# An MLP by Strassen's seven products, with hidden operands through DRAM

## The chip, the core and the metric

The kernel runs on one core of a Trainium2 chip. A core has a matrix engine (TensorE, PE in the profile; its weight loads are PEld), a vector engine (VectorE, DVE), a scalar engine (ScalarE, ACT), GpSimd (POOL) and a sync engine (SyncE, SP) whose queue issues most DMAs here. Each engine works through its own list of instructions in order and waits on semaphores of the others. The metric is device time in microseconds of one launch.

## The reference

One layer (`DEPTH` is 1) on 1024 rows of 1024 channels: a mixer of two recurrences, then an MLP with 4096 hidden channels, then a last norm. Everything is float32.

```python
for l in range(DEPTH):
    h = rms_norm(x, norm_mix[l])
    x = x + hybrid_mixer(h, ...)          # eight projections, two recurrences, gates, @ w_out
    h = rms_norm(x, norm_mlp[l])
    x = x + jnp.square(jax.nn.relu(h @ w_up[l])) @ w_down[l]
return rms_norm(x, norm_final)
```

`w_up` is 1024 x 4096, `w_down` 4096 x 1024. The change touches the MLP, the output projection of the second half of the rows and the norm between them.

## The kernel before

Time (1024 rows) is worked on in two chunks of `T` = 512. Products in float32 are made of three passes of the matrix engine: `split` (lines 72 to 74) makes a high part with a ScalarE copy into the type `float32r` (line 73) and a low part with a VectorE subtraction (line 74), and `mm3` (lines 113 to 116) issues high x high, high x low and low x high into one PSUM bank. So each operand that TensorE reads costs ScalarE and VectorE one pass, and each product of 128 x 128 x 512 costs three matmuls.

Weights lie in DRAM as tiles of 128 x 1024 floats (512 KB). `load_w` (line 79) puts a tile into one of three `raw` buffers by a DMA on SP's queue; `split_w` (line 84) makes the two parts, under a priority that puts it ahead of other work; `fill_w` and `get_w` (lines 96 and 103) run two tiles ahead of the use.

For each chunk the first norm is transposed and split into `hT`; four passes over channel groups run the projections, the recurrences and the gates and leave `y`, transposed and split. `out_proj` (line 598) multiplies `y` by `w_out`: for each half of 512 columns, four weight tiles, each used for two depth blocks and four blocks of 128 rows, so 192 matmuls for a chunk. For the second chunk it runs beside `second_norm(0)` (line 657), which norms the first chunk's rows, transposes them on TensorE into PSUM and splits them into `h20`; `second_norm(1)` then makes `h21` from the projection's results.

The MLP (from line 669) takes 512 hidden channels at a time, in eight blocks. For two groups of 256 channels it loads two tiles of `w_up` and two of `w_down`, forms `pu` in four PSUM banks (8 depth blocks x 2 chunks x 2 halves x 3 = 96 matmuls), and makes `u` = relu squared in two parts (lines 689 to 692). Then, for eight blocks of 128 rows, it forms `pd` in two banks (24 matmuls each) and VectorE adds it to `acc`, which holds the residual in SBUF (line 710). Up and down alternate block by block, and hidden values never leave SBUF. In the last block each row block is normed and stored as it ends (lines 711 to 722).

The order on each engine isn't the program's. A planner takes the traced program, with the order of the trace as priority (`high_priority(n)` moves a part up by n), and lists each engine's instructions by when it reckons their inputs and buffers to be ready; the chip then keeps that list. `tile_pool` hands out SBUF in stacks; a tag with `bufs=n` has n buffers that are used again when their last reader is done. PSUM has eight banks: tags `pj` (4), `sc` (2) and `hg` (2).

Of the kernel before, what the change touches and what calls it, by code (L numbers as in the profile page):

```python
# [10 lines left out]
F32 = mybir.dt.float32  # L11
# [7 lines left out]
P = 128  # L19
D = 1024  # L20
# [12 lines left out]
UP_TILES = 32  # L33
LEVELS = (2, 8)  # steps per segment; four segments are joined at a time

# columns of the per-channel parameters
# [5 lines left out]
def trunk(ctx: ExitStack, tc: tile.TileContext, x, wts, pv, gains, mask_f, mask_u, out):  # L42
# [4 lines left out]
    a2 = ctx.enter_context(tc.tile_pool(name="a2", bufs=4))  # L47
    wp = ctx.enter_context(tc.tile_pool(name="wp", bufs=3))
    ps = ctx.enter_context(tc.tile_pool(name="ps", bufs=1, space=PSUM))
    dram = ctx.enter_context(tc.tile_pool(name="dram", bufs=1, space=DRAM))  # L50

# [7 lines left out]
    up0 = MIX_TILES + OUT_TILES  # L59
    down0 = up0 + UP_TILES  # L60
    for b in range(8):
        seq += list(range(up0 + 4 * b, up0 + 4 * b + 4))
    ready, made = {}, [0]

    # at the start each engine's work goes in the order in which its inputs come in
# [10 lines left out]
    def raw_tile(name):  # L76
        return wp.tile([P, 1024], F32, tag="raw", name=name, bufs=3)
# [6 lines left out]
    def split_w(i, raw, pool, tag, bufs):  # L84
        h = pool.tile([P, 1024], F32R, tag=tag + "H", name=f"{tag}H{i}", bufs=bufs)
        lo = pool.tile([P, 1024], F32R, tag=tag + "L", name=f"{tag}L{i}", bufs=bufs)
        with tc.high_priority(400):
            split(raw, h, lo)
        return h, lo

    def load_split(i, pool, tag, bufs):
        return split_w(i, load_w(i), pool, tag, bufs)
# [3 lines left out]
    def fill_w(n):  # L96
        while made[0] < min(n, len(seq)):
            i = seq[made[0]]
            raw = raws.pop(0) if raws else load_w(i)
            ready[made[0]] = split_w(i, raw, wp, "w", 3)  # L100
            made[0] += 1
# [11 lines left out]
    def mm3(o, ah, al, bh, bl, first, last):  # L113
        PE.matmul(o, ah, bh, start=first, stop=False)  # L114
        PE.matmul(o, ah, bl, start=False, stop=False)  # L115
        PE.matmul(o, al, bh, start=False, stop=last)  # L116

# [30 lines left out]
    def a2_set(tag, name):  # L148
        return [
            [a2.tile([P, 4, T], F32R, tag=tag, name=f"{name}{q}{h}") for h in range(2)] for q in ("H", "L")  # L150
        ]
# [38 lines left out]
    def parameters():  # L190
        # softmax over the depth of one layer (exp(z) = sigmoid(z) / sigmoid(-z)), its running sum less the first, clipped
# [11 lines left out]
        # softplus(-lam) = max(-lam, 0) + 2 atanh(s / (2 - s)), s = sigmoid(-|lam|)  # L203
# [30 lines left out]
    def first_norm(c):  # L234
        dst = a2_set("h", f"hT{c}")
# [33 lines left out]
    def project(c, name):  # L269
        """256 channels, channels on partitions, a chunk of time along the free dimension."""  # L270
# [69 lines left out]
            # w = tanh(-log_a / 2): a = (1 - w) / (1 + w), sqrt(1 - a^2) = 2 sqrt(w) / (1 + w)  # L340
# [39 lines left out]
    def hgrn(c, p, q1, f, kk, v):  # L380
        """Two heads; decays from a step to the next are multiplied up, segment by segment."""
        nm = f"{c}{p}"
        mul = lambda o, a, b: V.tensor_tensor(out=o, in0=a, in1=b, op=ALU.mult)  # noqa: E731
# [3 lines left out]
        def blocks(rhs, name):  # L387
            """32 steps against themselves, 48 columns each."""
# [9 lines left out]
        # a step with itself and with the one before it in its pair  # L398
# [5 lines left out]
        # to segments of two  # L404
# [19 lines left out]
        for li, cw in enumerate(LEVELS):  # L424
# [13 lines left out]
            # decay from a segment's end to the last one's, and from the first one's start to a segment's  # L438
# [34 lines left out]
        # segments of 32, then of 64  # L473
# [41 lines left out]
        # the state at the start of each 128 steps, and what comes out  # L515
# [4 lines left out]
        for s in range(2):  # L520
# [7 lines left out]
            vn = lambda n: v[:, n, s * P : (s + 1) * P]  # noqa: B023, E731  # L528
# [3 lines left out]
            state = lambda n: scar[:, u, :] if n in (0, 4) else sn[:, n - 1, :]  # noqa: B023, E731  # L532
# [92 lines left out]
    for c in range(NC):  # L625
# [5 lines left out]
        ys = a2_set("y", f"y{c}")  # L631
# [15 lines left out]

# [1 line left out]
    late = ctx.enter_context(tc.tile_pool(name="late", bufs=1))  # L649
    gain1 = gain_tile(1)  # L650
    h2 = [a2_set("h", "h20")]
    acc = [late.tile([P, D], F32, tag="acc", name=f"acc{t}", bufs=8) for t in range(8)]
    for t in range(4):
        nc.sync.dma_start(acc[t], x2d[t])
        nc.sync.dma_start(acc[4 + t], x[(4 + t) * P : (5 + t) * P, :])
# [132 lines left out]
```

## Time and profile before

| | before |
|---|---|
| median of 3 runs | 1684.24 us (1683.9 to 1684.39) |
| profiled execution, first to last instruction (span) | 1682.1 us |
| of it before the second chunk's output projection | 926.7 us |
| last output projection, second norm, MLP, last norm | 755.4 us |
| instructions | 22982, of them 9624 matmuls |
| DMA moved | 133.24 MB, 79 GB/s in the mean |

The profile is of a single execution; its own time is given only as the span, and 2.1 us lie between that and the median of the runs. In the profile's lists a group of instructions has its line, engine, operation, the tile written and the tiles read (without buffer numbers), shapes, the number of instructions, then busy time in us and mean ns of one, then the idle time of the engine just before them with what ended it. A row of a window table is: from:to, length, then for PE, PEld, DVE, ACT and (where it worked) POOL the busy time in us with the number of instructions, then the granted clock, the DMA engines' busy share and GB/s. A row of the timeline is: start us, duration us, engine, line, operation, tiles, shapes, count, and in brackets what the engine had waited for.

### The profile page before, as it was taken

What the parts mean: (1) busy time and instruction counts of PE and PEld (TensorE: products, weight loads), DVE (VectorE), ACT (ScalarE), POOL (GpSimd) and SP (SyncE); (2) the same over time, 40 slices, a digit from 0 to 9 for tenths busy, and PEclk for the clock granted to TensorE, in tenths of its full rate; (3) what the DMA queues carried; (4) which work ended last, traced back from release to release, by engine and by line L of the source; (5) the groups of instructions that cost most, each with busy time, mean ns of one, the idle gap of its engine ahead of it and who ended that gap; (6) DMA issues with size and microseconds to landing.
All of it is one profiled execution on the core that took longest, in us unless ns stands there. A gap on an engine that the chain in (4) does not pass through costs nothing.

```text
span 1682.1 us, 22982 instructions
## 1 busy us (share of the span) xinstructions
PE 1652.1 (98%) x9624; PEld 1374.0 (82%) x9624; DVE 939.0 (56%) x1379; ACT 606.0 (36%) x974; POOL 61.8 (4%) x99
## 2 busy tenths in 40 slices
PE   7999999999999999999999999999999999999998
PEld 6788788787888787887887888888888888888886
DVE  5965947759646858658487663333424342424335
ACT  5534445435435435444363441212212121313132
POOL 0000100101000000000000000000000000000000
PEclk9999999999999999999999999999999999999999
DMA  6222222222353122122221531111111020202002
GB/s 217 88 72 92 89 76 89 76 89 87 101 172 116 64 93 96 65 87 88 86 90 64 188 112 38 53 49 38 63 38 63 26 75 26 75 26 76 26 0 100
DMA packets 38983, 133.24 MB, mean 79 GB/s; under 512 B 4576, under 2 KB 4704, under 8 KB 38880
## 3 DMA queue, kind: packets, MB, share of 16 engines
q1 hardware_dynamic: 38448, 130.21, 23.0%
q8 instruction: 75, 1.23, 0.3%
q10 hardware_dynamic: 432, 1.57, 0.3%
q14 instruction: 28, 0.23, 0.0%
HBM read 125.47 MB, written 6.29 MB: 78 GB/s over the span
## 4 chain that ended last, share of the span: by engine, by line
PE 84%; DVE 13%; issue 1%; DMA 1%; ACT 1%; POOL 0%; SPq 0%; DVEq 0%; POOLq 0%
PE pd L114 7%; PE pd L116 7%; PE pd L115 7%; PE pu L116 7%; PE pu L114 7%; PE pu L115 7%; DVE wL L74 2%; PE pj_ga L116 2%; PE pj_ga L115 2%; PE pj_ga L114 2%; PE pj_f L116 2%; PE pv L115 2%; PE pv L114 2%; PE pv L116 2%; PE pj_ma L116 2%; PE pj_ma L115 2%
## 5 line engine op out<-in xcount | busy, mean ns | idle before, releaser
L74 DVE TENSOR_TENSOR wL<-raw,wH 128x1024 fp32r<-128x1024 f32 x184 | 223.8, 1216 | 261.7 <-ACT wH L73 259.1
L73 ACT CAST wH<-raw 128x1024 fp32r<-128x1024 f32 x184 | 192.9, 1049 | 224.4 <-issue 65.4
L114 PE MATMUL pd<-dH,uH 128*128 128x512 f32 x512 | 199.2, 389 | 0.0
L115 PE MATMUL pd<-dL,uH 128*128 128x512 f32 x512 | 199.2, 389 | 0.0
L116 PE MATMUL pd<-dH,uL 128*128 128x512 f32 x512 | 199.2, 389 | 0.0
L710 DVE TENSOR_TENSOR acc<-pd,acc 128x512 f32<-128x512 f32 x128 | 87.2, 690 | 183.0 <-PE pd L116 183.0
L73 ACT CAST dH<-raw 128x1024 fp32r<-128x1024 f32 x32 | 33.6, 1052 | 281.7 <-PE pd L116 260.5
L116 PEld LDWEIGHTS pd<-dH,uL 128*128 128x128 f32 x512 | 96.1, 188 | 20.0
L115 PEld LDWEIGHTS pd<-dL,uH 128*128 128x128 f32 x512 | 96.1, 188 | 19.9
L114 PEld LDWEIGHTS pd<-dH,uH 128*128 128x128 f32 x512 | 96.1, 188 | 19.9
L691 DVE TENSOR_TENSOR r<-r 128x512 f32<-128x512 f32 x64 | 42.7, 686 | 114.8 <-ACT uH L690 114.8
L689 ACT ACTIVATE r<-pu 128x512 f32<-128x512 f32 x64 | 37.7, 591 | 176.3 <-PE pu L116 176.3
L115 PE MATMUL pu<-h20L,wH 128*128 128x512 f32 x256 | 99.9, 390 | 0.0
L114 PE MATMUL pu<-h20H,wH 128*128 128x512 f32 x256 | 99.8, 390 | 0.0
L115 PE MATMUL pu<-h21L,wH 128*128 128x512 f32 x256 | 99.6, 389 | 0.0
L116 PE MATMUL pu<-h20H,wL 128*128 128x512 f32 x256 | 99.6, 389 | 0.0
L116 PE MATMUL pu<-h21H,wL 128*128 128x512 f32 x256 | 99.6, 389 | 0.0
L114 PE MATMUL pu<-h21H,wH 128*128 128x512 f32 x256 | 99.4, 389 | 0.0
L115 PEld LDWEIGHTS pu<-h21L,wH 128*128 128x128 f32 x256 | 48.1, 188 | 10.0
L114 PEld LDWEIGHTS pu<-h21H,wH 128*128 128x128 f32 x256 | 48.1, 188 | 10.0
L116 PEld LDWEIGHTS pu<-h21H,wL 128*128 128x128 f32 x256 | 48.1, 188 | 10.0
L114 PEld LDWEIGHTS pu<-h20H,wH 128*128 128x128 f32 x256 | 48.1, 188 | 9.9
(297 smaller groups left out, 3701.4 us busy)
## 6 DMA issues: line engine op xcount, KB each, us to landing
raw<-wts_in SPq DMA_DIRECT2D x216, 512.0 KB, 3.5
x<-x_in SPq DMA_DIRECT2D x8, 512.0 KB, 5.5
y_out<-acc SPq DMA_DIRECT2D x16, 256.0 KB, 2.0
xs<-x_in SPq DMA_DIRECT2D x8, 256.0 KB, 3.0
x<-xs SPq DMA_DIRECT2D x8, 256.0 KB, 2.6
acc<-x SPq DMA_DIRECT2D x4, 512.0 KB, 6.9
acc<-x_in SPq DMA_DIRECT2D x4, 512.0 KB, 7.4
gain<-gains_in ACTq DMA_DIRECT2D x3, 512.0 KB, 5.0
```

The costliest lines, as they stand in the source:

```text
L73: keep(A.copy(h, src))
L74: keep(V.tensor_tensor(out=lo, in0=src, in1=h.bitcast(F32), op=ALU.subtract))
L114: PE.matmul(o, ah, bh, start=first, stop=False)
L115: PE.matmul(o, ah, bl, start=False, stop=False)
L116: PE.matmul(o, al, bh, start=False, stop=last)
L689: A.activation(r, pp[s][c], AF.Relu)
L691: V.tensor_tensor(out=r, in0=r, in1=r, op=ALU.mult)
L710: V.tensor_tensor(out=acc[t][:, cols], in0=pp[hf], in1=acc[t][:, cols], op=ALU.add)
```

## The change

The MLP's two products are each cut into 2 x 2 blocks of operands, and instead of eight block products seven are formed (in the form due to Strassen and Winograd), from sums of blocks. Because every operand is split into two parts after its sums are formed, each of the seven is again an `mm3`. `PLAN` lists the seven steps with a bank, a weight operand and an operand of the other side. Bank X is accumulated over four steps and read between them.

- *Weights.* A "quad" is four blocks of 128 x 512 floats (1 MB in two `raw` tiles), 16 for `w_up`, 16 for `w_down`. `sums` forms four sums on VectorE; `a`, `b`, `c`, `d` split the seven operands: A11 (512 wide), then s1 and s2, s3 and s4, A12 and A22 in pairs (1024 wide). High and low parts of the pairs share six buffers, one quad's worth.
- *Second norm.* The output projection of the second chunk runs in two parts of two row blocks, and the eight weight tiles pass twice. Each part is preceded by the norm of two row blocks of the first chunk and followed by that of its own. Beside copying the transposed values to SBUF, the norm of the first half splits B11 and B21; that of the second half splits B22, forms four sums (`combos`) and splits t1, n2, T3 and T4.
- *Up phase.* All 16 quads of the up product in turn. `hidden(q, step)` issues 12 matmuls; after steps 0 to 2 ScalarE copies the bank away, after 3 to 5 VectorE adds that copy to the bank, followed by Relu and Square; step 6 needs Relu and Square alone. `hidden_ops` makes the seven operands of the down product from the four blocks of results: 3.5 MB for a quad. For 14 of the 16 quads they are stored to DRAM; the last two stay.
- *Down phase.* Eight blocks of two quads each, in two halves of two row-block pairs. Each step's bank is added to or subtracted from `x2` (the residual in SBUF) by VectorE (`ADDS`). Each next block's weights are split beside the second half of a block, and `load_u` brings its operands back from DRAM. Quads with an even place use `ust` (one buffer of one operand, three of two operands), those with an odd place `late_u` (two and five).
- *Memory.* Pools are opened and closed by hand (`opened`), some at the far end of SBUF, so that later tiles take the place of earlier ones tile by tile; there are four raw buffers for three.

The diff, cut to its core:

```diff
+    def combos(b11, b21, b22, b12):
+        V.tensor_tensor(out=b11, in0=b11, in1=b12, op=ALU.subtract)
+        V.tensor_tensor(out=b12, in0=b22, in1=b12, op=ALU.subtract)
+        V.scalar_tensor_tensor(b22, b11, -1.0, b22, op0=ALU.mult, op1=ALU.subtract)
+        V.scalar_tensor_tensor(b21, b22, -1.0, b21, op0=ALU.mult, op1=ALU.subtract)
+    PLAN = (
+        ("X", "A11", "B11"), ("Y", "s1", "t1"), ("X", "s2", "n2"), ("Z", "A12", "B21"),
+        ("X", "s3", "T3"), ("Y", "s4", "B22"), ("X", "A22", "T4"),
+    )
+    BANK = {"X": "pj", "Y": "sc", "Z": "hg"}
...
+    for part in range(2):
+        tts = (2 * part, 2 * part + 1)
+        for tt in tts:
...
+            second_norm(tt, 0)
+        for hf in range(2):
+            pp = {tt: bank("pj", f"po1{hf}{tt}") for tt in tts}
+            for j in range(4):
+                wh, wl = next_w()
...
+        for tt in tts:
+            nc.sync.dma_start(x2d[4 + tt], x2s[tt])
+            second_norm(tt, 1)
...
+        def sums():
...
+            V.tensor_tensor(out=sa[:, 0, :], in0=a21, in1=a22, op=ALU.add)
+            V.tensor_tensor(out=sa[:, 1, :], in0=sa[:, 0, :], in1=a11, op=ALU.add)
+            V.tensor_tensor(out=sb[:, 0, :], in0=a21, in1=a11, op=ALU.add)
+            V.tensor_tensor(out=sb[:, 1, :], in0=sa[:, 1, :], in1=a12, op=ALU.add)
...
+    U_GROUPS = (("B11", "B21"), ("B22",), ("t1", "T4"), ("n2", "T3"))
...
+    def hidden(q, step):
+        bk, wo, ho = PLAN[step]
...
+        for k in range(4):
+            cols = slice(k * P, (k + 1) * P)
+            mm3(o, wh[:, cols], wl[:, cols], hh[:, k, :], hl[:, k, :], first and k == 0, k == 3, not first)
+        if step < 3:
...
+            A.copy(e_of[q, step], o)
+        elif step < 6:
+            at, e = {3: (0, 0), 4: (2, 1), 5: (3, 2)}[step]
+            V.tensor_tensor(out=b[:, at, :], in0=o, in1=e_of.pop((q, e)), op=ALU.add)
+            A.activation(b[:, at, :], b[:, at, :], AF.Relu, scale=-1.0 if at == 2 else 1.0)
+            A.activation(b[:, at, :], b[:, at, :], AF.Square)
+        else:
+            A.activation(b[:, 1, :], o, AF.Relu, scale=-1.0)
+            A.activation(b[:, 1, :], b[:, 1, :], AF.Square)
+    def hidden_ops(q, pool, many, keep_it):
...
+        def made(g, src):
+            t = u_tile(pool, q, g, many)
+            split(src, t[:, 0], t[:, 1])
+            if not keep_it:
+                nc.sync.dma_start(u_d[q, g], t.rearrange("p a b c -> p (a b c)").bitcast(F32))
+        made(U_GROUPS[0], b[:, 0:2, :])
+        made(U_GROUPS[1], b[:, 2:3, :])
+        combos(*(b[:, i, :] for i in range(4)))
+        made(U_GROUPS[2], b[:, 0:2, :])
+        made(U_GROUPS[3], b[:, 2:4, :])
+    for q in (0, 1):
+        load_quad(q)
...
+        hidden(q, 0)
+        hidden(q, 3)
...
+    for q in range(QUADS):
...
+        for step in range(7):
...
+            hidden(q, step)
...
+            if step == 1:
+                load_quad(n)
+            for k in {2: ("sums", "a", "b"), 5: ("c",), 6: ("d",)}.get(step, ()):
+                work[n][k]()
+        if q < QUADS - 1:
+            hidden_ops(q, ust, (1, 3), q == QUADS - 2)
...
+    hidden_ops(QUADS - 1, late_u, (2, 5), True)
...
+    with tc.high_priority(160):
+        load_quad(QUADS + order[1], raw_late)
+        w_late = work[QUADS + order[1]] = quad_steps(QUADS + order[1], side[1][0], raw_late)
+        for k in ("sums", "a", "b", "c", "d"):
+            w_late[k]()
+    for t in (0, 4, 1, 5, 2, 6, 3, 7):
+        nc.scalar.dma_start(x2[t], x2d[t])
...
+    for kb in range(n_kb):
+        last = kb + 1 == n_kb
+        qs = order[2 * kb : 2 * kb + 2]
+        for half in range(2):
+            pairs = (2 * half, 2 * half + 1)
...
+            alone = last and half == 1
+            for step, (bk, wo, uo), prs in [
+                (i, plan, prs) for prs in ([(pr,) for pr in pairs] if alone else [pairs]) for i, plan in enumerate(PLAN)
+            ]:
+                for pr in prs:
...
+                    for i, q in enumerate(qs):
...
+                        mm3(banks[bk, pr], uh[:, cut], ul[:, cut], wh, wl, first and i == 0, i == 1, not first)
+                for pr in prs:
+                    _, ci, cj, op = ADDS[step]
+                    dst = x2[pr + 4 * cj][:, ci * 512 : (ci + 1) * 512]
+                    V.tensor_tensor(out=dst, in0=dst, in1=banks[bk, pr], op=op)
...
+            if half == 1 and not last:
+                for i in range(2):
+                    load_u(order[2 * kb + 2 + i], *side[i][1:])
```

More of the change, by code (lines that the diff above doesn't have):

```diff
@@ L32 @@
 OUT_TILES = 8
-UP_TILES = 32
+QUADS = 16
 LEVELS = (2, 8)
@@ L58, in trunk @@
         seq += list(range(MIX_TILES + OUT_TILES))
[L59 to L62, printed above, removed]
+    seq += list(range(MIX_TILES, MIX_TILES + OUT_TILES))
     ready, made = {}, [0]
@@ L646, in trunk @@
     xt_cm.__exit__(None, None, None)
-    late = ctx.enter_context(tc.tile_pool(name="late", bufs=1))
-    gain1 = gain_tile(1)
[L651 to L655, printed above, removed]
-    def second_norm(c):
-        for tt in range(4):
-            t = 4 * c + tt
-            xn = late.tile([P, D], F32, tag="uH", name=f"xn_h{t}", bufs=4)
-            norm_rows(acc[t], xn, gain1, f"h{t}")
-            transposed(xn, h2[c], tt, f"h{t}")
@@ new lines, in trunk, with second_norm, op_split @@
+    h2p = [opened(f"h2{i}", side="right") for i in range(4)]
+    HOME = {"T4": 0, "B22": 0, "T3": 0, "B21": 1, "n2": 2, "t1": 2, "B11": 3}
+    n2p, close_n2 = opened("n2")
+    gain1 = gain_tile(1)
+    hop = {
+        o: [h2p[HOME[o]][0].tile([P, 4, T], F32R, tag=o + q, name=f"h2{o}{q}") for q in ("H", "L")]
+        for _, _, o in PLAN
+    }
+    x2s, braw = {}, {}
+    def second_norm(tt, half):
+        cut = slice(tt * P, (tt + 1) * P)
+        b = braw[tt, half] = n2p.tile([P, 2, T], F32, tag=f"b{half}", name=f"braw{tt}{half}", bufs=2 - half)
+        t = tt + 4 * half
+        xn = n2p.tile([P, D], F32, tag="xn", name=f"xn_h{t}", bufs=2)
+        if half == 0:
+            xs = n2p.tile([P, D], F32, tag="x2a", name=f"x2a{t}")
+            nc.sync.dma_start(xs, x2d[t])
+        else:
+            xs = x2s[tt]
+        norm_rows(xs, xn, gain1, f"h{t}")
+        def op_split(src, o):
+            split(src.rearrange("p (k t) -> p k t", k=4), hop[o][0][:, :, cut], hop[o][1][:, :, cut])
+        for h in range(2):
+            pt = bank("hg", f"xT_h{t}_{h}")
+            for k in range(4):
+                PE.transpose(pt[:, k * P : (k + 1) * P], xn[:, (4 * h + k) * P : (4 * h + k + 1) * P], ident)
+            A.copy(b[:, h, :], pt)
+            if (half, h) != (1, 0):
+                op_split(b[:, h, :], {(0, 0): "B11", (0, 1): "B21", (1, 1): "B22"}[half, h])
+        if half == 1:
+            b0 = braw[tt, 0]
+            combos(b0[:, 0, :], b0[:, 1, :], b[:, 1, :], b[:, 0, :])
+            for src, o in ((b0[:, 0, :], "t1"), (b[:, 1, :], "n2"), (b[:, 0, :], "T3"), (b0[:, 1, :], "T4")):
+                op_split(src, o)
@@ new lines, in trunk, with u_tile @@
+    ust, close_ust = opened("ust")
+    up, close_up = opened("up")
+    U_GROUPS = (("B11", "B21"), ("B22",), ("t1", "T4"), ("n2", "T3"))
+    u_d = {
+        (q, g): dram.tile([P, 2 * len(g) * T], F32, tag=f"u{q}{g[0]}", name=f"u{q}{g[0]}")
+        for q in range(QUADS - 2)
+        for g in U_GROUPS
+    }
+    u_ops = {}
+    work, b_of, bank_of, e_of = {}, {}, {}, {}
+    def u_tile(pool, q, g, many):
+        t = pool.tile([P, 2, len(g), T], F32R, tag=f"u{len(g)}", name=f"u{q}{g[0]}", bufs=many[len(g) - 1])
+        u_ops[q].update({o: (t[:, 0, j, :], t[:, 1, j, :]) for j, o in enumerate(g)})
+        return t
@@ new lines, in raw_late, with load_u @@
+    def raw_late(name):
+        return late_raw.tile([P, 1024], F32, tag="raw", name=name, bufs=4)
+    def load_u(q, pool, many):
+        u_ops[q] = {}
+        for g in U_GROUPS:
+            t = u_tile(pool, q, g, many)
+            nc.sync.dma_start(t.rearrange("p a b c -> p (a b c)").bitcast(F32), u_d[q, g])
+    n_kb = QUADS // 2
+    order = [QUADS - 2, QUADS - 1] + list(range(QUADS - 2))
+    side = [((w1p, wp), ust, (1, 3)), ((late_w1, late_w), late_u, (2, 5))]
+    raw_of = (raw_tile, raw_late)
```

241 lines of the change are left out of this document (162 added, 79 removed).

## The prediction

> **What bounds the kernel now.** I read the page first (engine shares, slices, chain), then the windows of the stretch that the change touches, then the groups by line for the price of each kind of instruction, and last the timeline at the two seams.
>
> ```profile
> span 1682.1 us, 22982 instructions
> PE 1652.1 (98%) x9624; PEld 1374.0 (82%) x9624; DVE 939.0 (56%) x1379; ACT 606.0 (36%) x974; POOL 61.8 (4%) x99
> PE   7999999999999999999999999999999999999998
> DVE  5965947759646858658487663333424342424335
> PE 84%; DVE 13%; issue 1%; DMA 1%; ACT 1%; POOL 0%; SPq 0%; DVEq 0%; POOLq 0%
> ```
>
> TensorE is busy in every slice and carries 84% of the chain. The DVE line falls from 6 to 8 tenths to 3 or 4 after slice 23: that is the MLP, where VectorE has room. A busy PE is not PE at its peak, so the pace comes from counts:
>
> ```profile
> 988.00:1670.00 682.00, 681.97 (x3012) 564.86 (x3013) 249.61 (x339) 146.88 (x222) 0.00 (x0) 1.00 0.15 49
> L114 PE MATMUL pu<-h20H,wH 128*128 128x512 f32 x256 | 99.8, 390 | 0.0
> L114 PE MATMUL pd<-dH,uH 128*128 128x512 f32 x512 | 199.2, 389 | 0.0
> 926.72 0.48 PE L114 MATMUL po<-wH,y1H 128*128 128x512 f32 x1
> 976.98 1.06 PE L144 MATMUL xT_h<-ident,xn_h 128*128 128x128 f32 x8
> 1675.09 0.39 PE L116 MATMUL pd<-dH,uL 128*128 128x512 f32 x1
> ```
>
> In 682 us of pure MLP, 3012 matmuls start: **0.2264 us each**, for both products (equal durations, 390 and 389 ns). As a test over the whole stretch from the first matmul of the last output projection (926.7): 192 of these (43.5), 64 transposes at 1.06 for 8 (8.5) and 3072 MLP matmuls (695.5) would end at 1674.2; the last one ends at 1675.5. So TensorE loses about 1.3 us in 749: the MLP is bound by the number of matmuls, and 6.6 us of tail follow the last one.
>
> **The change part by part.** *Matmuls.* Before: 8 blocks x 384 = 3072. After: up 16 quads x 7 products x 12 = 1344, down 8 blocks x 2 halves x 7 x 12 = 1344, together 2688. Their shapes are the old ones, so 384 x 0.2264 = **-86.9 us**. What remains is whether the other engines can feed this pace: 84 matmuls, 19.0 us, for a quad of the up phase; 168, 38.0 us, for a block of the down phase.
>
> ```profile
> L74 DVE TENSOR_TENSOR wL<-raw,wH 128x1024 fp32r<-128x1024 f32 x184 | 223.8, 1216 | 261.7 <-ACT wH L73 259.1
> L692 DVE TENSOR_TENSOR uL<-r,uH 128x512 fp32r<-128x512 f32 x64 | 42.8, 688 | 1.2
> L310 DVE SCALAR_TENSOR_TENSOR xc<-xp,pvt,xc 128x512 f32<-128x512 f32 x48 | 33.1, 746 | 0.0
> L710 DVE TENSOR_TENSOR acc<-pd,acc 128x512 f32<-128x512 f32 x128 | 87.2, 690 | 183.0 <-PE pd L116 183.0
> L73 ACT CAST wH<-raw 128x1024 fp32r<-128x1024 f32 x184 | 192.9, 1049 | 224.4 <-issue 65.4 <-PE pu L115 52.0 <-PE po L116 37.0
> L689 ACT ACTIVATE r<-pu 128x512 f32<-128x512 f32 x64 | 37.7, 591 | 176.3 <-PE pu L116 176.3
> L690 ACT ACTIVATE uH<-r 128x512 fp32r<-128x512 f32 x64 | 40.3, 632 | 1.5
> 850.00:900.00 50.00, 48.60 (x430) 38.63 (x429) 45.05 (x73) 26.18 (x35) 3.55 (x6) 1.00 0.25 85
> ```
>
> *Up phase, VectorE per quad:* four weight sums 4 x 0.688 = 2.75; low parts of the weights 0.69 + 3 x 1.216 = 4.34; three bank additions 2.07; low parts of the hidden operands 3 x 1.216 + 0.69 = 4.34; `combos` 2 x 0.688 + 2 x 0.746 = 2.87. Sum **16.4 of 19.0 us**. *ScalarE:* eight high parts 7.5, three bank copies 1.8, four Relu 2.4, four Square 2.5: 14.2. *Down phase, VectorE per block:* 28 additions 19.3 and two quads' weights 14.2: **33.5 of 38.0**. Both are 86 to 88%, and the row at 850 shows VectorE busy for 45.05 of 50 us (90%) while PE is busy for 48.6. So PE keeps the lead, with little to spare. An addition that ends late hits PE directly, since a bank X is read between two of its own products. It has one step, 2.7 us, for the rest of an earlier instruction (1.22 at most) and its own 0.69. I charge 5 us to the up phase (0.3 a quad) and 7 to the down phase (0.9 a block). The ends are 0, and VectorE usable only 80% of the time: 1.5 more a quad and 3.9 more a block, 55 in all. I take values near the low end, since 90% is nearest.
>
> *DRAM.* Each quad stores 3.5 MB of operands and loads 1 MB of weights in 19.0 us; each block loads 7 MB and 2 MB in 38.0 us: 248 GB/s both times.
>
> ```profile
> 10.00:20.00 10.00, 8.28 (x50) 7.16 (x49) 7.07 (x11) 6.89 (x13) 1.41 (x3) 1.00 1.02 375
> raw<-wts_in SPq DMA_DIRECT2D x216, 512.0 KB, 3.5
> 926.07 0.69 DVE L594 TENSOR_TENSOR sma<-g,sma 128x512 f32<-128x512 f32 x1 [2.04 <-ACT sma L591]
> 926.68 0.74 DVE L586 SCALAR_TENSOR_TENSOR g<-poT,pvt,g 128x512 f32<-128x512 f32 x1
> ```
>
> At the start the 16 engines, fully busy, moved 375 GB/s, so the average fits (two thirds). Timing matters in one place. A block's reloads reuse the previous block's buffers. `ust` has three two-operand buffers, freed after steps 3, 4 and 6 of the last half. Two can thus be refilled early; the third holds the operands of step 2, two steps (5.4 us) after it is freed. 512 KB land in 3.5 us, so 1 MB in about 3.5 + 1.4 = 4.9: just in time, at nothing. Without that cover it costs the excess, seven times. This needs the planner to queue loads by when their buffers come free. For VectorE it does so: L594 ran before L586, which stands earlier in the program. For SP's queue no row shows it.
>
> *First seam.* The last output projection is walked twice, two row blocks at a time, so its eight weight tiles are loaded and split again. The second norm now also forms seven operands. PE's own count is unchanged.
>
> ```profile
> L138 DVE SCALAR_TENSOR_TENSOR xn_h<-acc,rstd_h,gain 128x1024 f32<-128x1024 f32 x8 | 10.3, 1284 | 3.0 <-POOL rstd_h L137 2.7
> 952.00:978.00 26.00, 25.85 (x129) 21.21 (x130) 14.16 (x20) 11.00 (x16) 0.55 (x1) 1.00 0.26 81
> 973.48 1.06 ACT L135 ACTIVATE xn_h<-acc 128x1024 f32<-128x1024 f32 x1 [3.13 <-DVE acc L612]
> 974.66 0.15 DVE L136 TENSOR_SCALAR rstd_h<-rstd_h 128x1 f32<-128x1 f32 x1
> 975.55 1.29 DVE L138 SCALAR_TENSOR_TENSOR xn_h<-acc,rstd_h,gain 128x1024 f32<-128x1024 f32 x1
> ```
>
> After the last projection matmul VectorE needs for two row blocks: additions 1.4, norms 2.6, B22 1.4, `combos` 5.7, eight low parts 5.5, together 16.6, behind 2.1 of Square and root (973.5 to 975.6): 18.7, of which the last 2 may follow PE's restart. PE has 48 matmuls that need only first-half operands (10.9) and 16 transposes (2.1). Floor: 18.7 - 2 - 13.0 = 4 us. Before the projection ends, PE's 43.5 + 6.4 us face on VectorE: 16 weight splits 19.5, six additions 4.1, six norms 7.7, eight half-one splits 5.5, two second halves 12.6, the mixers' leftover some 6.5, and the first quads' weights 7.8: 64. So up to 14 us are in arrears: top 18. I take **12**, nearer the top, since these 14 cannot all be started late. VectorE was busy for only 14.2 of 26 us here; that cover is what the change uses up.
>
> *The clock after a long wait.*
>
> ```profile
> 9.42 1.97 PE L144 MATMUL xT_x<-ident,xn 128*128 128x128 f32 x8 [9.42 <-DVE xn L138]
> 12.75 0.41 PE L116 MATMUL pv<-wH,hT0L 128*128 128x256 f32 x1
> 12.96 0.41 PE L114 MATMUL pv<-wH,hT0H 128*128 128x256 f32 x1
> 15.35 1.07 PE L144 MATMUL xT_x<-ident,xn 128*128 128x128 f32 x8 [0.92 <-DVE xn L138]
> 16.74 0.28 PE L114 MATMUL pv<-wH,hT0H 128*128 128x256 f32 x1
> 16.85 0.28 PE L115 MATMUL pv<-wL,hT0H 128*128 128x256 f32 x1
> ```
>
> After 9.4 us of idleness eight transposes took 1.97 us and matmuls followed at 0.21; some 4 us later 1.07 and 0.11, after a gap of 0.9 that cooled nothing. So a long wait costs about 0.9 + 11 x 0.1 = **2.0 us** more; I charge one, for the first seam. [...]
>
> *Second seam.* The last quad's operands are the first that the down phase needs. The chain after the last up matmul is Relu 0.59, Square 0.63, high part 1.05, low part 1.22, less 0.7 of the other quad's matmuls: 2.8. Then t1 behind 0.69 + 2.87 + 1.05 + 1.22 = 5.8 against step 0's 2.7: 3.1 more. Floor 6. In that last quad VectorE also makes one more quad's weights (7.1): 23.5 in 19.0 us, so top 6 + 4.5. I take **9**. *The end:* the last half takes its row blocks one by one, with additions due within 1.35 us: 1. *Before 926 us* nothing is added but pool layout and an extra raw buffer: 0, within 5 either way, as the planner may order anew.
>
> **Sum:** 1682.1 - 86.9 + 5 + 7 + 12 + 2 + 9 + 1 = 1631.2 span. The median of the runs shown is 1684.24, 2.1 above the profiled span: **1633 us**.
>
> **The rivals.** *Seams hidden:* both at their floor, phases without loss: 1595.2 + 4 + 6 = 1605 span, 1607. For it: VectorE overlaps neighbours (974.66 to 975.55 holds three instructions). Against it: 64 us of work in 50. *VectorE sets the pace* in both phases, 80% usable: 1633 - 12 + 55 = 1676. For it: 88% asked, and ping-pong with ScalarE in every split; in the table above VectorE idled 259 us waiting for that very copy. Against it: the 90% row.
> *Slower: the reloads stand in line.*
>
> ```profile
> SPq L81 <- DVE wL L74: 950.3, 157, 18.4
> ```
>
> SP's queue stood 950 us at its head, waiting for weight buffers; whatever is behind waits along. If a block's loads are queued in program order, the third buffer's wait for step 6 holds up all 3.5 MB of the second quad. Its first operands then land 4.9 + 2.8 = 7.7 us after step 6, needed at 0.7; its t1 lands at 11.9, needed at 10.4. That is 7.0 + 1.5 a block, and 2.0 of cold clock: 10.5 x 7 = 73, giving 1706. It decides from some 7 us a block (1684 - 1633 = 51, over 7). That the change doesn't do what it says is no case here: the loops fix the count of matmuls.
>
> **How the numbers follow.** Forecast 0.57; seams hidden 0.15; VectorE's pace 0.15; reloads in line 0.10; seams and phases both at their tops (1595.2 + 55 + 18 + 10.5 + 2 + 1 = 1682 span, 1684, no change) 0.03. 0.2%, 3.4 us, is about what a measurement tells from no change. Faster 0.57 + 0.15 + 0.15 = 0.87, same 0.03, slower 0.10. The range runs from just under the first rival to just over the second: 1602 to 1680; outside it lie the slower case, the near-no-change case and the fringes, under 2 in 10.
>
> **What would show it.** Right: 384 fewer matmuls; in the up windows about 443 matmuls in 100 us, as before, with VectorE at 85 to 90%; one PE gap of 10 to 15 us between 975 and 1005, waiting for t1 or another hidden operand; some 9 us in pieces between the phases, 304 us of up matmuls later. Wrong: in the list of waits, PE behind DMA on the reloaded `u` tiles (the slower rival), PE behind VectorE's bank additions in every block (the second), or no gap at the seams (the first).

## The result and the profile after

The changed kernel takes **1632.8 us** (1631.69 to 1635.1, four runs) beside 1684.32 us for the kernel before on the same chip: ratio 0.9696 [0.9683, 0.971]. The forecast was 1633. The profiled execution has a span of 1631.6 us, forecast 1631.2. The sum came out almost exactly; but two of its terms came out for another reason than the one given, one was far too high, and several smaller losses were not in it.

The page of the changed kernel, the rows that answer to those of before (totals, VectorE's 40 slices, the chain):

```profile
span 1631.6 us, 23177 instructions
PE 1585.5 (97%) x9240; PEld 1301.9 (80%) x9240; DVE 1212.6 (74%) x1751; ACT 762.4 (47%) x1186; POOL 63.9 (4%) x99
DVE  5975956848764965848759688977777887888876
PE 81%; DVE 14%; DMA 2%; issue 1%; ACT 1%; POOL 0%; DVEq 0%; POOLq 0%; SPq 0%; ACTq 0%
```

9240 is 9624 - 384: the matmuls went as counted. VectorE, which had been busy for 3 or 4 tenths of the MLP, now stands at 7 or 8, and TensorE still carries 81% of the chain. The windows of the changed kernel, two of the steady phases and the two seams (columns as before: from:to, length, busy us and number of instructions of PE, PEld, DVE, ACT, POOL, granted clock, DMA share, GB/s; the number takes in those that are already running when the window begins):

```profile
976.00:985.00 9.00, 3.44 (x20) 2.51 (x19) 8.52 (x14) 4.82 (x9) 1.31 (x2) 0.86 0.44 175
985.00:990.00 5.00, 4.55 (x20) 3.65 (x19) 3.83 (x7) 4.35 (x9) 0.96 (x2) 0.58 0.41 126
1000.00:1012.00 12.00, 10.32 (x45) 7.87 (x43) 8.85 (x14) 7.44 (x13) 0.00 (x0) 1.00 0.01 2
1050.00:1150.00 100.00, 100.00 (x430) 80.28 (x429) 78.67 (x97) 69.86 (x98) 0.00 (x0) 1.00 0.64 250
1300.00:1310.00 10.00, 10.00 (x45) 8.12 (x44) 10.00 (x12) 7.19 (x11) 0.00 (x0) 1.00 0.79 266
1310.00:1320.00 10.00, 9.13 (x38) 6.56 (x37) 10.00 (x16) 5.55 (x9) 0.00 (x0) 1.00 0.89 359
1380.00:1480.00 100.00, 100.00 (x433) 80.87 (x432) 81.55 (x116) 18.50 (x20) 0.00 (x0) 1.00 0.68 270
```

The same two stretches of the kernel before, both within its MLP:

```profile
1050.00:1150.00 100.00, 100.00 (x443) 82.84 (x442) 34.03 (x45) 18.10 (x25) 0.00 (x0) 1.00 0.13 43
1380.00:1480.00 100.00, 100.00 (x443) 82.84 (x442) 34.43 (x46) 17.29 (x24) 0.00 (x0) 1.00 0.14 43
```

Read the counts, not the busy time: TensorE is "busy" for 100.00 of 100 us everywhere, yet the changed kernel has 430 matmuls in the up phase and 433 in the down phase, where 443 had been forecast (and were there before). Taken pair by pair from the traces, a matmul starts 233.3 ns after the one before it in the up phase and 231.9 ns in the down phase, instead of 226.7; this time from start to start is called the interval below. Who makes it wait? The list of PE's waits (engine, line, what it waited for, us in total, times, longest) of the changed kernel, without the rows of the first norm and the mixer:

```profile
PE xT_h L701 <- DVE rstd_h L137: 6.2, 2, 5.6
PE xT_h L701 <- DVE xn_h L139: 1.9, 4, 0.9
PE uX L115 <- ACT ws30H L76: 1.7, 1, 1.7
PE uZ L115 <- ACT braw L702: 1.1, 1, 1.1
PE dX L115 <- DMA u0n<-u0n: 1.0, 1, 1.0
PE dZ L116 <- DVE wA1230L L77: 0.9, 1, 0.9
PE uX L117 <- DVE wA L77: 0.5, 1, 0.5
PE xT_h L701 <- ACT h2B11H L76: 0.5, 1, 0.5
PE dX L115 <- DVE acc L960: 0.4, 1, 0.4
```

Nobody. Of all VectorE's additions out of banks in both phases one held up TensorE, once, for 0.4 us. The reloads through DRAM held it up once, for 1.0 us. The first four rows and the two of 0.5 are the first seam; the weights of the late block (0.9) are the second. The slower pace has no wait behind it at all, and that became the question.

The first seam in the timeline of the changed kernel (start us, us, engine, line, operation, count, in brackets idle time before it and what ended it):

```profile
977.05 0.33 SPq L690 DMA_DIRECT2D x2a<-x  x1
...
980.49 1.06 ACT L136 ACTIVATE xn_h<-x2a 128x1024 f32<-128x1024 f32 x1
...
983.06 1.28 DVE L139 SCALAR_TENSOR_TENSOR xn_h<-x2a,rstd_h,gain 128x1024 f32<-128x1024 f32 x1 [0.44 <-POOL rstd_h L138]
...
984.49 1.94 PE L701 MATMUL xT_h<-ident,xn_h 128*128 128x128 f32 x8 [5.56 <-DVE rstd_h L137]
```

TensorE waits 5.56 us for the norm of one row block, whose rows were only loaded at 977.05 because `x2a` has one buffer. Then eight transposes take 1.94 us, where they had taken 1.06, and the windows show the granted clock at 0.86 and 0.58: 6.8 us at half pace in the trace's record (982.4 to 989.2).

### The profile page after: what moved, and what is told of

It is laid out like the page before. It is cut to its first block, busy times and chain, and to the rows that moved or that the text cites. A ratio compares the mean times of both kernels' runs of the same rounds, so it can differ in the third digit from the quotient of the medians.

```text
span 1631.6 us, 23177 instructions
## 1 busy us (share of the span) xinstructions
PE 1585.5 (97%) x9240; PEld 1301.9 (80%) x9240; DVE 1212.6 (74%) x1751; ACT 762.4 (47%) x1186; POOL 63.9 (4%) x99
## 4 chain that ended last, share of the span: by engine, by line
PE 81%; DVE 14%; DMA 2%; issue 1%; ACT 1%; POOL 0%; DVEq 0%; POOLq 0%; SPq 0%; ACTq 0%
PE dX L115 4%; PE dX L117 3%; PE dX L116 3%; PE uX L117 3%; PE uX L115 3%; PE uX L116 3%; DVE wL L77 2%; PE pj_ga L117 2%; PE pj_ga L116 2%; PE pj_ga L115 2%; PE pj_ma L117 2%; PE pj_f L117 2%; PE pv L116 2%; PE pv L115 2%; PE pv L117 2%; PE pj_ma L116 2%
## 5 line engine op out<-in xcount | busy, mean ns | idle before, releaser
L960 DVE TENSOR_TENSOR acc<-acc,dX 128x512 f32<-128x512 f32 x128 | 87.0, 685 | 35.1 <-PE dX L117 34.1
L960 DVE TENSOR_TENSOR acc<-acc,dY 128x512 f32<-128x512 f32 x64 | 43.8, 685 | 19.9 <-PE dY L117 18.0
L345 DVE RECIPROCAL rr<-rr 128x512 f32<-128x512 f32 x16 | 53.5, 3347 | 0.0
L820 ACT ACTIVATE b<-b 128x512 f32<-128x512 f32 x48 | 30.3, 632 | 38.8 <-DVE b L819 38.7
L115 PE MATMUL pv<-wH,hT0H 128*128 128x256 f32 x128 | 37.1, 289 | 0.2 <-ACT wH L76 0.2
L116 PE MATMUL pv<-wL,hT0H 128*128 128x256 f32 x128 | 36.7, 287 | 0.0
L117 PE MATMUL pv<-wH,hT0L 128*128 128x256 f32 x128 | 36.7, 286 | 0.0
L115 PE MATMUL pv<-wH,hT1H 128*128 128x256 f32 x128 | 36.5, 285 | 0.0
L116 PE MATMUL pv<-wL,hT1H 128*128 128x256 f32 x128 | 36.2, 283 | 0.0
L117 PE MATMUL pv<-wH,hT1L 128*128 128x256 f32 x128 | 36.2, 283 | 0.0
L821 ACT ACTIVATE b<-b 128x512 f32<-128x512 f32 x48 | 30.0, 630 | 1.1
```

Source lines behind the costliest of these rows:

```text
L115: PE.matmul(o, ah, bh, start=first, stop=False, **how)
L116: PE.matmul(o, ah, bl, start=False, stop=False, **how)
L117: PE.matmul(o, al, bh, start=False, stop=last, **how)
L345: V.reciprocal(rec, rec)
L820: A.activation(b[:, at, :], b[:, at, :], AF.Relu, scale=-1.0 if at == 2 else 1.0)
L821: A.activation(b[:, at, :], b[:, at, :], AF.Square)
```

## The experiments

**Is it the place in SBUF? First try: 64 bytes.** In the changed kernel the tiles at the far side of SBUF start 32 bytes past a multiple of 64; in the kernel before all operands of these matmuls start at multiples of 64. One edit aligns them, the other (the line with `const`) takes the alignment from the kernel before. Here and below the edits are cut to their core.

```diff
+    rpad, close_rpad = opened("rpad", side="right")
+    G.memset(rpad.tile([P, 8], F32, tag="pad", name="pad"), 0.0)
     h2p = [opened(f"h2{i}", side="right") for i in range(4)]
...
+    G.memset(const.tile([P, 8], F32, tag="pad", name="pad"), 0.0)
```

> The changed kernel, with one 32-byte tile put first at the far end of SBUF, so that every tile there (all operands of the second norm, the second side of the down phase) starts at a multiple of 64 bytes instead of 32 bytes past one. Nothing else changes. Theory A, the start address sets the pace: matmul intervals fall from 0.2333 us (up) and 0.232 us (down) to the 0.2267 us of before, 1344 x 0.0067 + 1344 x 0.0052 = 16 us less, about 1617 us. Theory B, PE loses this time at the bank additions of VectorE, as the prediction charged it (5 + 7 us): intervals and time unchanged, 1633 us. Theory C, the DRAM traffic slows the operand reads: also unchanged.

> The kernel before, with one 32-byte tile put first among its constants, so that all its matmul operands start 32 bytes past a multiple of 64. It has no Strassen steps, no added DRAM traffic and VectorE idle for 60% of the MLP. Theory A: intervals of the MLP go from 0.2267 to 0.2333 us, 3072 x 0.0067 = 20 us more, and up to 3264 x 0.0067 = 22 us more for the 512-wide matmuls of the mixer and projections; 1705 to 1727 us. Theories B and C: 1684 us, unchanged.

Measured: 1632.66 us (0.9693 [0.968, 0.9707]) and 1684.42 us (1.000 [0.9991, 1.001]); the intervals stayed at 233.3 and 231.8, and at 226.7. That theory fell. (What the two runs did not test shows below.)

**The gap of the first seam.** Two `x2a` buffers, the norm in place, and one `xn` buffer.

```diff
-            xs = n2p.tile([P, D], F32, tag="x2a", name=f"x2a{t}")
-            nc.sync.dma_start(xs, x2d[t])
+            xn = n2p.tile([P, D], F32, tag="x2a", name=f"x2a{t}", bufs=2)
+            nc.sync.dma_start(xn, x2d[t])
+            norm_rows(xn, xn, gain1, f"h{t}", b.rearrange("p a b -> p (a b)"))
```

> The changed kernel, with two buffers for the rows that the second norm of the first chunk reads back (one before), and that norm done in place so that it fits. Theory D, the 5.6 us wait of PE at the first seam is that one buffer (reload issued at 977.05, Square at 980.49, transposes at 984.49): the wait falls under 2 us and the half clock behind it (6.8 us, about 2 us of loss) goes, 4 to 6 us less, about 1628 us. Theory E, the wait is VectorE's arrears, as the prediction worked it out: the operands are ready at the same time and the end moves by under 1 us.

> Both edits together. If they are independent, as A and D have it, the sum of the two gains: 1633 - 16 - 5 = 1612 us. If the faster pace only moves the wait (VectorE then has 19.0 us a quad instead of 19.6), some of the 16 us comes back as waits for VectorE in the list.

Measured: 1635.86 us (0.9715 [0.9702, 0.9729]) and, with the 32 bytes too, 1636.37 us (0.9714 [0.9701, 0.9728]): by the medians 3 us slower than the changed kernel, not faster. The waits of the first, and a window of it:

```profile
PE xT_h L701 <- DVE xn_h L139: 8.2, 4, 4.4
PE xT_h L701 <- DVE x2a L139: 3.2, 2, 2.7
PE xT_h L701 <- DVE rstd_h L137: 0.7, 1, 0.7
```

```profile
985.00:990.00 5.00, 4.78 (x16) 4.13 (x17) 4.41 (x9) 3.39 (x7) 0.00 (x0) 0.50 0.00 0
```

The wait for the reload went (6.2 to 0.7) and came back as 11.4 us for the norms themselves, which had been 1.9. Up products start 1.7 us earlier (986.8 for 988.5), but the trace's record of the clock now has two stretches of 6.8 us at half pace at the seam, where the changed kernel has one (granted clock over the whole run 0.994 for 0.997). The seam is bound by more than that buffer; whether the single `xn` buffer or VectorE's arrears hold it now was not taken apart.

**Is it the order of banks?** In the traces of both kernels, intervals just after a gap are mostly 229 to 236 ns and turn to 227 after a few matmuls in the projections, but never in the recurrent products (six in a row into one bank) nor in the changed up phase (twelve). So the next theory was that only frequent switches of PSUM bank bring the pace back.

```diff
-            hidden(q, step)
+            if q > 1 and step == 0:
+                continue
+            hidden(q, step, *((q + 1, 0) if step == 6 and 0 < q < QUADS - 1 else ()))
```

(`hidden` with four arguments issues the two steps' groups of three in turn.) In the down phase:

```diff
-                for pr in prs:
-                    for i, q in enumerate(qs):
+                for i, q in enumerate(qs):
+                    for pr in prs:
```

And the reverse in the kernel before:

```diff
-                for k in range(8):
-                    for s in range(2):
+                for s in range(2):
+                    for k in range(8):
...
-            order = [(k, hf) for hf in range(2) for k in range(4)] if last else [(k, hf) for k in range(4) for hf in range(2)]
+            order = [(k, hf) for hf in range(2) for k in range(4)]
```

> The changed kernel, with one edit in the up phase: the last step of a quad (bank X of that quad) and the first step of the next quad (another bank X) issue their matmuls alternately, three into the one bank and three into the other, eight groups in each of 14 quads. Work, operands and every other step are as they were. Theory R (a start-to-start interval of 233 ns is the state of the PE after any interruption, and only a few switches of PSUM bank at every third matmul bring it to 227 ns; once there it stays): in the traces of both kernels the intervals after each gap are 230 to 236 ns and turn to 227 after two to four such switches, while in runs of 12 in one bank they never do. Then the up phase goes to 226.7 ns from about the third quad on, 1224 matmuls x 6.6 ns = 8 us less, 1624.5 us; the down phase stays at 231.9. Rival O (the interval belongs to what the new operands and the accumulation into standing banks are): 233.3 ns all through and 1632.8 us. Rival S (the small interruptions of 50 ns at every second quad throw it back each time): half of the gain, 1628 to 1629.

> The changed kernel, with one edit in the down phase: a step walks its two quads outside and its two row blocks (two banks) inside, so that banks alternate at every third matmul instead of at every sixth. The last half block keeps runs of six and twelve. Theory R: 231.9 goes to 226.7 ns in the down phase, 1344 x 5.2 ns = 7 us less, less a few for the start: 1626 us; the up phase stays at 233.3. Rival O: 1632.8 us. A cost against it: a bank's last matmul comes 0.7 us later before the VectorE addition that reads it, with 4 us until the bank is written again, so nothing.

> Both edits of the two runs before it together. Theory R: both phases at 226.7 ns, 8 + 7 = 15 us less, 1618 us. Rival O: 1632.8 us.

> The kernel before, with the order of its MLP matmuls alone changed: the up product walks one bank to its end (24 matmuls) before the next, and every down product 12 in one bank and 12 in the other, where all but the last block alternated at every third matmul. Same matmuls, operands, flags and copies. Theory R: the PE comes out of the transposes of the second norm at the slow interval and never meets the switches that mend it: 233 ns in all 3072 MLP matmuls, 3072 x 6.6 = 20 us more, 1704.5 us. Rival O, and any cause that lies in the new kernel's operands or transfers: 226.7 ns and 1684.3 us. In between, if runs of 24 and 12 hold a pace but do not make it: 1684 to 1704, with the place of the change visible in the trace.

Measured: 1634.12 us (0.9702 [0.9687, 0.9716]), 1630.36 us (0.9679 [0.9665, 0.9693]), 1632.12 us (0.9691 [0.9676, 0.9705]) and 1683.83 us (0.9996 [0.9987, 1.0006]). The kernel before with 12 to 24 matmuls in a row into one bank kept its pace, its window as full as ever:

```profile
1050.00:1150.00 100.00, 100.00 (x443) 82.81 (x442) 34.77 (x45) 17.86 (x24) 0.00 (x0) 1.00 0.13 43
```

and the changed up phase with switches at every third matmul kept its own (430 in 100 us). The bank theory fell too. But the down phase with the loops exchanged did gain, 437 in 100 us for 433 (the 2.4 us less in the median alone would not tell the two apart, as their 95% ranges overlap):

```profile
1380.00:1480.00 100.00, 100.00 (x437) 81.64 (x436) 82.64 (x118) 19.32 (x20) 0.00 (x0) 1.00 0.70 277
```

What the exchange also halves is how often the two quads alternate, whose operands lie on the two sides of SBUF. In the down phase of the changed kernel three or more intervals in a row of at most 228 ns come twelve times, and ten of these runs end at such a change of sides. So: place after all, but another rule than 64 bytes.

**Moving the weights.** One word in each kernel puts the pool of split weights at the far side (in the changed kernel the line has `bufs=1`).

```diff
-    wp = ctx.enter_context(tc.tile_pool(name="wp", bufs=3))
+    wp = ctx.enter_context(tc.tile_pool(name="wp", bufs=3, side="right"))
```

> The kernel before, with one word added: the pool of the split weights lies at the far end of the SBUF (199 to 223 KB of a partition) and no longer in its middle (98 to 121 KB). Same instructions in the same order. Theory H (the interval goes by where a matmul's two operands lie: 227 ns where moving and stationary operand lie in the same part of the SBUF, 233 ns where the one lies in the low and the other in the high part, and a switch of both from one part to the other throws a fast run back). In the traces so far the recurrent products (moving operand at 178 to 185 KB, weights at 98 KB) run at 233 ns in the kernel before too, every product of the changed up phase has its moving operand at 112 to 223 KB and its weights at 18 to 51 KB, and in the down phase each fast run ends where both operands change sides. Then the projections, the output projection and the up products of this run (2688 + 384 + 1536 = 4608 matmuls, one operand at 21 to 85 KB, the other at 199 to 223 KB) go to 233 ns: up to 4608 x 6.6 = 30 us more, 1709 to 1715 us; the down products (117 to 179 KB both) stay at 227. Rival O (place is nothing): 1684.3 us and 226.7 ns.

> The changed kernel with the same one word. In its up phase moving operands now lie at 71 to 181 KB and the weights at 199 to 223 KB (those of A11 alone stay at 6 to 14 KB). Theory H: the products of T4, T3, B22 and B21 (moving at 119 to 181 KB) go from 233.3 towards 227 ns, 5 to 9 us less; the projections and the output projections (one operand at 6 to 68 KB, the other at 199 to 223 KB) go to 233 ns, 3072 x 6.6 = up to 20 us more; the recurrent products (126 to 132 KB, 199 KB) to 227 ns; the down phase, where the even quad now has its operands on both sides, some 2 us more. 1641 to 1650 us in all, but what decides is the interval of each group. Rival O: 233.3 ns in the up phase, 226.7 in the projections, 1632.8 us.

Measured: 1704.26 us (1.012 [1.0103, 1.0137]) and 1636.17 us (0.9714 [0.9699, 0.9728]). The same instructions of the kernel before, with the weights elsewhere, cost 20 us: the last output projection starts 8.9 us later (935.6 for 926.7; part of what the projections lose lies beside waits, hence less than the 30 us of the expectation), and the up products lose 10. Its windows, the first in an up product, the second in a down product, whose operands did not change sides:

```profile
1084.00:1118.00 34.00, 34.00 (x148) 27.34 (x147) 13.70 (x17) 11.97 (x17) 0.00 (x0) 1.00 0.19 62
1124.00:1158.00 34.00, 34.00 (x152) 28.16 (x151) 10.35 (x16) 0.14 (x1) 0.00 (x0) 1.00 0.05 16
```

148 against 152 matmuls in 34 us (the interval is 233.3 ns in the mean of all up products, 226.9 in the down products). In the changed kernel the reverse happened: the up phase rose from 430 to 439 in 100 us, more than expected, and the projections slowed; the time of 1636 us is below the 1641 to 1650 that was expected.

```profile
1050.00:1150.00 100.00, 100.00 (x439) 81.96 (x438) 81.70 (x103) 69.65 (x99) 0.00 (x0) 1.00 0.66 257
```

Place it is. But the theory with sides (near and far) did not hold in detail: in the second of these runs t1, with its moving operand at 87 to 101 KB and weights at 211 to 217 KB, ran at 227 ns, while A11, with 71 to 85 KB and 6 to 14 KB, alone stayed at 233. Each matmul in the trace has a moving operand (128 x 512, named first) and a stationary one (128 x 128, named second, for which the trace has a weight load of PEld, 0.19 us, that begins before the matmul). In the up phase the weights are the stationary operand, in the down phase the moving one. Sorted by the difference between the start address of a matmul's moving operand and that of the next matmul's stationary operand, modulo 512 bytes (addresses from the compiled programs, mean interval from the traces, 512-wide matmuls, intervals of 245 ns and more counted as gaps and left out):

| kernel | products | difference mod 512 | matmuls | mean ns |
|---|---|---|---|---|
| before | down | 0 | 1535 | 226.7 |
| before | projections (with the matmuls just after gaps) | 0 | 2543 | 227.6 |
| before | recurrent | 448 | 177 | 233.2 |
| changed | up | 224 | 1325 | 233.3 |
| changed | down, within a side / at changes of side | 0 / 224, 288 | 923 / 409 | 231.0 / 233.8 |
| changed, 32 bytes (first try) | up | 192 | 1325 | 233.3 |
| before, weights moved | up; projections | 96 | 4062 | 233.4 |
| before, weights moved | down | 0 | 1528 | 226.9 |
| changed, weights moved | up without A11 | 0 | 1122 | 227.1 |
| changed, weights moved | A11 | 224 | 187 | 233.0 |

A difference of 0 runs at 227 ns once up to ten in a row are past; no group with another difference has a mean under 230 ns in any of these traces. In the down phase of the changed kernel each matmul's own two operands agree modulo 512 all through, so it is the stationary operand of the next matmul that goes with the pace. All this is read from these traces and addresses alone; what in the chip makes it so, no run shows. The first try had moved the difference from 224 to 192 and, in the kernel before, moved everything alike: neither touched it.

**The rule, tried.** 224 bytes on the far side make every difference in the MLP 0; 96 bytes make it 128 in the up phase, which tells the modulus. In the second run a further edit, in the down phase, keeps SyncE's queue to program order for the reloads: the slower rival of the prediction.

```diff
+    G.memset(rpad.tile([P, 56], F32, tag="pad", name="pad"), 0.0)
```

For 96 bytes the tile has 24 floats. The reloads in program order:

```diff
-            nc.sync.dma_start(t.rearrange("p a b c -> p (a b c)").bitcast(F32), u_d[q, g])
+            tc.keep_in_program_order(nc.sync.dma_start(t.rearrange("p a b c -> p (a b c)").bitcast(F32), u_d[q, g]))
```

> The changed kernel with one 224-byte tile put first on the far side of the SBUF, so that every tile there starts 224 bytes lower. Theory M (the two runs with the moved weights, read again: what tells 227 from 233 ns is neither side nor distance but whether the start address of the moving operand that streams and that of the next stationary operand are equal modulo a power of two between 128 and 512 bytes). Over ten runs, pairs with difference 0 mod 512 ran at 226.7 ns once three or more came in a row, and no pair with another difference (32, 64, 96, 160, 192, 224 mod 256) ever did. With 224 bytes the difference is 0 in every MLP matmul, switches of side too (the run with 32 bytes had left it at 192). Theory M: 226.7 ns in both phases but for some ten matmuls after each gap, 1344 x 6.6 + 1344 x 5.2 = 16 us less, 1617 us (1616 to 1619). Theory H (the part of the SBUF): 233.3 and 231.9 as before, 1632.8 us.

> Two edits that meet in no phase, read apart in the trace. (1) The far-side tile has 96 bytes, so the difference in the up phase is 128 mod 512. If the modulus of theory M is 128, the up phase runs at 226.7 ns; if it is 256 or 512, at 233.3. (2) In the down phase SyncE's queue is kept to program order for the reloads, the even quad's four before the odd quad's four: the slower rival of the prediction, which charged 7.0 + 1.5 us of waiting and 2.0 of slow clock a block, 73 us in seven blocks, beside the order by free buffers of the changed kernel, which waits 1 us in all. By the rival's sum 1632.8 + 72 = 1705 us (9 less if the modulus is 128), with the PE waiting for reloaded tiles at the start of each block. If the transfers land early enough in any order, no such wait and 1633.

Measured, first run: **1620.06 us**, 0.9618 [0.9602, 0.9634] of the kernel before, 12.7 us less than the changed kernel by nothing but 224 unused bytes, with a span of 1618.4 us. Its windows:

```profile
1050.00:1150.00 100.00, 100.00 (x441) 82.29 (x440) 81.23 (x101) 71.60 (x103) 0.00 (x0) 1.00 0.65 250
1380.00:1480.00 100.00, 100.00 (x443) 82.84 (x442) 81.95 (x119) 17.75 (x20) 0.00 (x0) 1.00 0.65 258
```

443 in 100 us again in the down phase, 441 in the up phase (each second quad a small hiccup starts some ten matmuls at the slow interval). Means 227.0 and 226.8 ns. Its compiled program has the same matmuls in the same order as the changed kernel's. Summed over the pairs in the MLP, what intervals take beyond 226.7 ns fell from 15.6 to 0.6 us, nearly the 16 us expected; 2.2 us of that came back as longer gaps (9.1 to 11.4 us in sum, the waits for `ws30H` and for the one reload among them). This is the best of all kernels run.

Second run: 1662.35 us, 0.9872 [0.9857, 0.9886]. The up phase stayed at 430 matmuls in 100 us (232.8 ns), so 128 is not the modulus: it is 256 or 512, and nothing here tells these two apart. (1024 it is not: in the kernel before 2986 matmuls with a difference of 0 modulo 1024 run at 227.2 ns and 2976 with 512 at 227.1.) In the down phase TensorE waits for the odd quad's first operand in each of the seven blocks; waits, then windows of the first block:

```profile
PE dX L115 <- DMA u7B<-u7B: 3.3, 1, 3.3
PE dX L115 <- DMA u11B<-u11B: 3.3, 1, 3.3
PE dX L115 <- DMA u9B<-u9B: 3.1, 1, 3.1
PE dX L115 <- DMA u1B<-u1B: 3.0, 1, 3.0
PE dX L115 <- DMA u5B<-u5B: 2.8, 1, 2.8
PE dX L115 <- DMA u13B<-u13B: 2.0, 1, 2.0
PE dX L115 <- DMA u3B<-u3B: 1.9, 1, 1.9
```

```profile
1354.70:1358.20 3.50, 0.45 (x3) 0.01 (x2) 2.70 (x5) 0.00 (x0) 0.00 (x0) 1.00 1.01 421
1358.20:1361.60 3.40, 3.40 (x8) 2.68 (x9) 1.20 (x2) 0.00 (x0) 0.00 (x0) 0.51 1.02 431
```

19.4 us of waiting in all, and after five of the seven waits a stretch at half the clock (8 matmuls in 3.4 us, granted clock 0.51). Together the run is 29.5 us above the changed kernel, 4.2 a block: the rival's mechanism at the rival's place, at 40% of the 10.5 it was charged, and still faster than the kernel before. The order alone costs some 2 us more than that, by an estimate from the intervals, since the 96 bytes made them shorter (up 233.3 to 232.8 ns, down within a side 231.0 to 229.9).

## Why the prediction was right, and where it was not

| step of the sum | on record | in the changed kernel |
|---|---|---|
| 384 matmuls fewer | -86.9 | 9624 to 9240, as counted |
| up phase, "late additions" | +5 | 8.7 (6.6 ns a matmul), not from VectorE |
| down phase, "late additions" | +7 | 6.9 (5.2 ns a matmul), not from VectorE |
| first seam and cold clock | +12, +2 | some 15.5 (what the others and the stretch ahead of it leave) |
| second seam | +9 | 1.8 |
| the reloads | 0 | 1.2 |
| the end | +1 | 1.7 (0.7 of gaps, 1.0 of longer tail) |

The gaps are counted as what a pair of matmuls takes beyond 226.7 ns.

*The matmuls.* Right, and the whole of the gain: what bounds the MLP is the number of matmuls, and the other engines could follow. (The 3012 of the working are matmuls in the window, not starts, so 0.2264 is 0.2267 pair by pair: 0.1 us in the term.)

*"An addition that ends late hits PE directly"*, 5 and 7 us. This is the step that failed. The amount is nearly right (16 for 12), the cause is wrong: TensorE waited 0.4 us for an addition in the whole down phase, and VectorE, busy for 79 to 82 of 100 us in the windows where 86 to 88% had been added up, had the room that the 90% row had promised. What takes the 16 us is the start-to-start interval itself, 233.3 and 231.9 ns for 226.7, which depends on where the operands lie. The run with 224 bytes takes 15 us of it away, 12.7 of them in the time, and changes nothing else but for one memset. The trace of the kernel before already had it, though no row of the prediction shows it: the recurrent products ran at 233 ns there. Equal durations (390 and 389 ns) were taken as proof that shape alone sets the pace, and the price of a matmul was carried to new tiles at new addresses without asking whether it would hold there.

*First seam*, 12 + 2. Right in place and in total, not in form. Forecast was one gap of 10 to 15 us that waits for t1 or another hidden operand; the trace has one of 5.6 us at 978.9 that waits for a norm, half clock for 6.8 us, then 1.1 and 1.7 and small pieces. The bounds of 4 and 18 held, and so did taking a value near the top; the rival of hidden seams, at its floor of 4, did not come. But the longest wait came from a buffer that was not in the sum (one `x2a`), and freeing it only moved the wait, which fits VectorE's arrears but was not taken apart: why the total is what it is stays open. The cold clock was charged as 2.0; half pace for 6.8 us, with TensorE not always at work, is up to 3.4.

*Second seam*, 9. Too high: 1.8 us. VectorE is busy for 10.00 of 10 us in both windows around 1310, as the 23.5 us of work in 19 had it, but the planner let matmuls of the other quad, whose operands were ready, run ahead, so TensorE has 38 in the second of these windows, with 0.9 us of waiting for the last weights. The floor of 6 assumed step order within a quad pair; nothing forced it.

*The reloads*, charged at nothing. Nearly right: a wait of 1.0 us, once. The condition named, that the planner queue the loads by when their buffers come free, held: in the changed kernel the odd quad's loads for free buffers go ahead of the even quad's that wait for step 6 (three of `u3` are issued from 1349.5 on, `u2` only from 1380.6 to 1388.8). Forcing program order shows what this order is worth, some 30 us. The rival's price was too high: of the 4.2 us a block, 2.8 are these waits, for 8.5 charged, and up to 1.5 the clock (20.5 us at half pace in all), for 2.0. The DMA engines moved 421 to 431 GB/s in that stretch (375 was assumed), and the planner put steps of the even quad in front; how much each took off was not taken apart.

*VectorE sets the pace*, the rival at 1676: in the windows VectorE's idle fifth remains in both phases, and of its additions one is waited for, 0.4 us long. No run loaded VectorE further, so how much room there is was not tried.

So the sum was right to 0.4 us partly by luck: 3.6 too little for the pace, 1.5 for the first seam, 1.2 for the one reload, 0.7 each for the end and for the stretch ahead of the projection (its first matmul starts at 927.4 for 926.7), 0.3 for small gaps within the up phase, 8 in all, against 7.2 too much for the second seam and 0.3 in the count of matmuls and the losses of before. Of the signs that were to show the mechanism, the count of matmuls came; 443 in 100 us, VectorE at 85 to 90%, the single long gap and the 9 us between the phases did not.

## What to carry to other kernels

When a matmul's price from one part of a kernel is used for another, compare counts per window, not durations. For 512-wide `float32r` matmuls as here, look whether each moving operand and the next stationary operand start at addresses that agree modulo 512 bytes: here groups that agree ran at 226.7 to 227.6 ns a matmul where they were not broken up, groups that don't at 232.8 to 233.8. A padding tile that makes them agree gave 0.8% here, and a pool moved carelessly cost 1.2%. A list of waits that is empty beside a pace that is slow says that the price of the instruction itself has changed. Where buffers are refilled through one queue, the order of the queue by free buffers, not by use, was worth some 30 us.

## What the hardware showed beside this

- The interval has a memory: after a gap the first matmuls start 228 to 234 ns apart in the mean even where addresses agree, and settle at 226.7 after some three to ten (means over the gaps of the kernel before). Twelve in a row into one bank don't disturb that (443 in 100 us above); a single change to operands with another difference does: in the changed down phase the intervals that follow one have means of 232.0 and 230.6 ns, though their own difference is 0.
- The length of a wait does not tell by itself whether half clock follows. In the run with the reloads in program order (windows of two blocks):

```profile
1530.20:1533.80 3.60, 0.64 (x3) 0.19 (x1) 3.60 (x7) 0.00 (x0) 0.00 (x0) 1.00 1.02 428
1533.80:1537.20 3.40, 3.13 (x12) 2.21 (x13) 1.49 (x3) 0.00 (x0) 0.00 (x0) 1.00 1.01 426
1617.30:1619.80 2.50, 0.47 (x3) 0.05 (x1) 0.00 (x0) 0.00 (x0) 0.00 (x0) 1.00 0.97 405
1619.80:1624.30 4.50, 4.50 (x13) 3.23 (x14) 1.38 (x2) 0.00 (x0) 0.00 (x0) 0.65 1.04 440
```

A pause of 3.5 us from start to start (1530.5 to 1534.0) was not followed by half clock (12 matmuls in 3.4 us at a granted clock of 1.00), one of 2.4 (1617.4 to 1619.8) was (13 matmuls in 4.5 us at 0.65). What decides it, no run here shows.
